# Grouped reads of shared PSUM banks, and a builder's clock that knows of bank turns

## The chip, the cores and the metric

The kernel runs on one core of one Trainium2 chip. The metric is the device time of one execution in microseconds (us). On a core, TensorE (PE; its weight loads are PEld), VectorE (DVE), ScalarE (ACT) and GpSimd (POOL) each work through their own list of instructions in order and wait for one another by semaphores; SyncE (SP) issues transfers. Matmul results land in PSUM, eight banks, from where only ACT and DVE read them.

## What is computed

One step of a decoder layer with two mixers on the same input: 256 prompt tokens and 8 sequences of 8 sample tokens, 320 columns in all, model width 2048.

```
h   = rms_norm(x) * (1 + scale) + shift            # scale, shift, gate from c @ w_ada
a_qkv, a_z, ..., b_z, i_q, ..., g_a, g_b = split(h @ w_in)
y_a = rms_norm(gated_delta_rule(conv(a_qkv))) * silu(a_z)       # 32 heads, states of 128 x 128
y_b = attend(q, k, v, top-k of an indexer) * silu(b_z)          # 16 heads, paged cache for the samples
out = rms_norm((sigmoid(g_a) * (y_a @ w_pa) + sigmoid(g_b) * (y_b @ w_pb)) @ w_out)
y   = x + gate * out

# the delta rule, chunk by chunk (128 tokens in the kernel, two chunks of prompt):
u = u_c - w_c @ s;   o = qd_c @ s + qk_c @ u;   s = s * g_tail + k_tail^T @ u
```

## The kernel before

**The stream.** All large products are weight-stationary. A weight matrix is loaded in tiles `raw` of 1024 rows by 256 columns (three buffers, issued on SP). A *unit* is 128 columns of one such half: ACT rounds it into `whi` (L334), DVE subtracts to get `wlo` (L335), three buffers of each, and PE runs 24 matmuls of 320 columns into one of two banks `pm`: input high part by `whi`, low part by `whi`, high part by `wlo`, for eight row blocks. Two units make a block of 128 output channels, and its `..._done` function reads the bank. The stream runs in the order: indexer queries, queries, gate `b_z`, gate `g_a`, then eight groups for the delta rule (keys, queries, `a_z`, values), gate `g_b`, and the three output projections.

**Side work.** Everything else is a Python generator ("side"). The other six banks, `ps`, are a ring that the sides take and give back; in the delta-rule stage one of them holds the short convolution. `stream` calls `side_round` twice in each unit, after 12 and after 24 matmuls (L364, L370), and each side whose time has come issues one step. The instructions of a step go to the end of each engine's list at that moment, so the order of the calls is the order on every engine.

**The clock.** When a side's time has come is decided by `Clock`, a table of estimated times that the builder keeps while it emits instructions. `Clock.enter` gives each instruction a start, the latest of its engine's time, its inputs' writers and its output's users, and an end. A step's end is stored with the side; `side_round` steps it again when the estimated time of PE has passed it:

```
if side[1] <= clock.t["tensor"]:
    self.step(side)
```

So a cost that the clock leaves out makes a step come early in the program, and PE then waits for it on the chip.

**Waits for a bank.** The framework under the kernel sets the semaphores. Between an ACT instruction and a DVE instruction on the same bank it sets one also where both only read, and where they read different columns.

**The places.** In `prompt_chain` (one for each of 16 pairs of heads) five blocks follow one another, each with a bank of its own: (1) `XT` by `vt[0]`, read by ACT into `wf` (a part of `vt`) and by DVE into `wt` (a tile `w`), for two heads v; (2) the state `S1` (also a tile `w`) and an output `ot`, read by ACT; (3) `kq` by `S1`, read by DVE into `x1` (a part of `vt`) and by ACT into `ot`; (4) `XT` by `x1`, read as in (1); (5) the new state. `sample_chain` has a block like (1) whose bank is read by DVE into `wt` and by ACT into `ot`, and then 16 DVE instructions, each shown as `S<-S,gtr,ps`. The chains of two pairs of heads run side by side. `bz_done` reads a `pm` bank twice, by DVE into `u` and by ACT (tanh) into `t`; both are tiles `t`. At that time DVE also runs the samples' top-k on `scs`, 32 rounds of two instructions. `out_done` reads its bank by ACT into `gsx`, by DVE into the rest of `gsx`, and by ACT into `sqx`. A PE row `pm<-...` belongs to the stream, `ps<-...` to the sides. All instructions go through one helper and carry its line, L56.

Of the kernel before, what the change touches and what calls it, by code (L numbers as in the profile page):

```python
# [11 lines left out]
AF = mybir.ActivationFunctionType  # L12
OP = mybir.AluOpType
AX = mybir.AxisListType
MEM = bass.MemoryType
# [5 lines left out]
NT = NP + NS  # L21
# [46 lines left out]
class Clock:  # L68
# [2 lines left out]

    def __init__(self):
        self.t = dict.fromkeys(("tensor", "vector", "scalar", "gpsimd", "sync", "dma"), 0.0)
        self.written, self.used = {}, {}
        self.last = 0.0

    @staticmethod
# [70 lines left out]
    def enter(self, name, op, args, kw):  # L148
        out = args[0] if args else kw["out"]
        rest = list(args[1:]) + list(kw.values())  # L150
        ins = [a for a in rest if hasattr(a, "tensor") and a is not out and a is not kw.get("accum_out")]
        outs = [out] + ([kw["accum_out"]] if kw.get("accum_out") is not None else [])
        if op == "transpose":
            ins = ins[:1]
        own = None if "dma" in op else name
        start = max(self.t[name], self.ready(*ins, name=own))
        if "dma" not in op or out.space != MEM.DRAM:
            start = max(start, self.idle(*outs, name=own))
        if "dma" in op:
            side = out if out.space != MEM.DRAM else ins[0]  # L160
            rows = self.free(side) // min(out.shape[-1], ins[0].shape[-1])
            size = side.shape[0] * rows * max(512, 4 * min(out.shape[-1], ins[0].shape[-1]))
            self.t[name] = start + (1.0 if name == "gpsimd" else 0.55)
            self.t["dma"] = max(self.t["dma"], start) + size / 3.2e5
            end = max(self.t["dma"], start) + 2.2
        else:
            if kw.get("op") == OP.pow or OP.pow in rest:
                took = 1.6
            else:
                took = self.cost(name, op, outs, ins)  # L170
            end = self.t[name] = start + took
            end += 0.2 if name == "tensor" else 0.1
        by = "dma" if "dma" in op else name
        for a in ins:
            self.note(self.used, a, by, end)
        for a in outs:
            self.note(self.written, a, by, end)
        self.last = max(self.last, end)
# [12 lines left out]
class Kernel:  # L191
# [809 lines left out]
    def bz_done(self, p, h):  # L1001
        self.force(lambda: h in self.att and len(self.t_r.free) >= 2)
        u, t = self.t_r.get(), self.t_r.get()
        self.ts(u, p[:, :NT], 0.5, None, OP.mult)
        self.act(t, p[:, :NT], AF.Tanh, scale=0.5)
        y = self.ybuf[:, h, :]
        self.stt(y[:, NP:NT], t[:, NP:NT], 1.0, u[:, NP:NT], OP.add, OP.mult)
        self.stt(u[:, 0:NP], t[:, 0:NP], 1.0, u[:, 0:NP], OP.add, OP.mult)
        self.tt(y[:, 0:NP], y[:, 0:NP], u[:, 0:NP], OP.mult)
        self.t_r.put(u)  # L1010
        self.t_r.put(t)
        if h == KB - 1:
            self.flags.add("bz")
# [730 lines left out]
    def prompt_chain(self, h, G):  # L1744
        nc, o = self.nc, self.o
        e, hv, K = h % 2, 2 * h, self.K[h]
        while "T" not in G or "vt" not in K:
            yield
        kq, vt, kt, XT, PT = K["kq"], K["vt"], K["ktok"], G["XT"], K["PT"]
        s, stl = self.scal(G, e)  # L1750
        yield self.ready(vt, XT)
        yield from self.need(self.ps_side)
        yield from self.need(self.w, 2)
        if "ot" not in K:
            yield from self.need(self.ot)
            K["ot"] = self.ot.get()
        ot = K["ot"]
        wt, S1 = self.w.get(), self.w.get()
        wf, x1 = vt[:, 0], vt[:, 1]
        p = self.psum()  # L1760
        for v in range(2):
            self.mm(p[:, 128 * v:128 * v + 128], XT[:, 4 * e + 2 * v, :], vt[:, 0, v, :])
        for v in range(2):
            self.act(wf[:, v, :], p[:, 128 * v:128 * v + 128], AF.Copy, scale=s(v, 0))
            self.ts(wt[:, v, :], p[:, 128 * v:128 * v + 128], stl(v, 0), None, OP.mult)
        self.ps_side.put(p)
        yield
        yield from self.need(self.ps_side)
        p = self.psum()
        self.mm(p[:, 0:256], kt[:, 0, :], wt)  # L1770
        for v in range(2):
            self.mm(p[:, 256 + 128 * v:384 + 128 * v], PT[:, v, 0, :], wf[:, v, :])
        self.act(S1, p[:, 0:256].rearrange("p (v d) -> p v d", v=2))
        self.act(ot[:, 0], p[:, 256:512].rearrange("p (v d) -> p v d", v=2))
        self.ps_side.put(p)
        yield
        yield from self.need(self.ps_side)
        p = self.psum()
        self.mm(p[:, 0:256], kq[:, 0, 128:256], S1)
        self.mm(p[:, 256:512], kq[:, 1, 128:256], S1)  # L1780
        for v in range(2):
            hc = hv + v
            self.stt(x1[:, v, :], p[:, 128 * v:128 * v + 128], self.neG[:, 1, hc:hc + 1], vt[:, 1, v, :], OP.mult, OP.add)
            self.act(ot[:, 1, v, :], p[:, 256 + 128 * v:384 + 128 * v], AF.Copy, scale=self.eG[:, 1, hc:hc + 1])
        self.ps_side.put(p)
        yield
        yield from self.need(self.ps_side)
        p = self.psum()
        for v in range(2):
            self.mm(p[:, 128 * v:128 * v + 128], XT[:, 4 * e + 2 * v + 1, :], x1[:, v, :])  # L1790
        for v in range(2):
            self.act(x1[:, v, :], p[:, 128 * v:128 * v + 128], AF.Copy, scale=s(v, 1))
            self.ts(wt[:, v, :], p[:, 128 * v:128 * v + 128], stl(v, 1), None, OP.mult)
        self.ps_side.put(p)
        yield
        yield from self.need(self.ps_side)
        p = self.psum()
        self.mm(p[:, 0:256], kt[:, 1, :], wt)
        for v in range(2):
            self.mm(p[:, 256 + 128 * v:384 + 128 * v], PT[:, v, 1, :], x1[:, v, :])  # L1800
        for v in range(2):
            self.stt(S1[:, v, :], S1[:, v, :], self.gtp[:, 1, hv + v:hv + v + 1], p[:, 128 * v:128 * v + 128],
                     OP.mult, OP.add)
        self.tt(ot[:, 1], p[:, 256:512].rearrange("p (v d) -> p v d", v=2), ot[:, 1], OP.add)
        self.ps_side.put(p)
        self.PT.put(PT)
        self.store(o[5][0, 0, hv:hv + 2].rearrange("h k v -> k h v"), S1, self.w)
        self.w.put(wt)
        self.drop_vt(K)
        self.drop_T(G)  # L1810
        K["P"] = True
# [6 lines left out]
    def sample_chain(self, h, G):  # L1818
# [11 lines left out]
        s, stl = self.scal(G, e)  # L1830
# [20 lines left out]
        p = self.psum()  # L1851
        for v in range(2):
            self.mm(p[:, 128 * v:128 * v + 128], XT[:, 8 + 2 * e + v, :], xr[:, v, :])
        for v in range(2):
            self.ts(wt[:, v, :], p[:, 128 * v:128 * v + 128], stl(v, 2), None, OP.mult)
        self.act(ot[:, 2], p[:, 0:256].rearrange("p (v d) -> p v d", v=2))
        self.ps_side.put(p)
        self.drop_T(G)
        yield
# [199 lines left out]
    def out_done(self, p, k):  # L2059
        self.force(lambda: self.gsx.free and self.sqx.free)  # L2060
        g, s = self.gsx.get(), self.sqx.get()
        self.act(g[:, :NP], p[:, :NP], AF.Copy, scale=self.gatp[:, k, 0:1])
        self.tt(g[:, NP:NT].rearrange("p (b t) -> p b t", t=TS), p[:, NP:NT].rearrange("p (b t) -> p b t", t=TS),
                self.gatp[:, k, 1:9].rearrange("p (b o) -> p b o", o=1).to_broadcast([128, NB, TS]), OP.mult)
        self.act(s, p[:, :NT], AF.Square)

        def gen():
            yield self.ready(g, s)
            p = self.psum()
            for t in range(3):  # L2070
                n = 128 if t < 2 else 64
                self.mm(self.pss[:n, t:t + 1], s[:, 128 * t:128 * t + n], self.one, start=(k == 0 and t == 0),
                        stop=(k == KB - 1), skip=True)
                self.tr(p[:n, 128 * t:128 * t + 128], g[:, 128 * t:128 * t + n])
            for t in range(3):
                n = 128 if t < 2 else 64
                self.act(self.gt[t][:n, 128 * k:128 * (k + 1)], p[:n, 128 * t:128 * t + 128])
            self.ps_side.put(p)
            self.gsx.put(g)
            self.sqx.put(s)  # L2080
            yield
        self.spawn(gen())
# [52 lines left out]
```

## Time and profile before

| | us |
|---|---|
| median of 3 runs | 2323.8 (2316.94 to 2326.34) |
| the profiled execution, device time | 2320.82 |
| its span, first to last instruction | 2319.1 |
| PE idle in the span (2319.1 less 2216.6 busy) | 102.5 |

The times above are of whole executions; all trace times are from the start of the span. Three matmuls of the stream are in flight at a time, so that each is shown longer (0.31 us) than the distance to the next (0.15 us). In a list of waits, `PE ps <- ACT w` means: a PE instruction that writes a `ps` bank was held, and the last thing it waited for was an ACT instruction that writes a tile `w`.

### The profile page before, as it was taken

The page shows a single profiled execution, that of the slowest core. Times are in us where ns is not written, and L with a number is a line of the kernel's source. Part 1 is how long each engine was busy: PE and PEld are TensorE (multiplying, and loading weights), DVE is VectorE, ACT ScalarE, POOL GpSimd, SP SyncE. Part 2 cuts the span into 40 slices and gives each one's busy share as a digit, 9 for nine tenths or more (in the row PEclk, how much of TensorE's full clock was granted, in tenths as well). Part 3 has the DMA queues.
Part 4 walks back from the last instruction along what each step waited for, and adds up shares of the span by engine and source line. Part 5 has one row for each costly group of instructions (what it writes and reads, how often), then busy time and mean ns, then how long its engine had stood idle before and what let it go on. Part 6 is the DMA issues. An engine that isn't in the chain of part 4 may idle for free.

```text
span 2319.1 us, 41332 instructions
## 1 busy us (share of the span) xinstructions
PE 2216.6 (96%) x16448; PEld 2081.1 (90%) x16448; DVE 1368.6 (59%) x2666; ACT 1013.4 (44%) x2191; POOL 469.4 (20%) x624
## 2 busy tenths in 40 slices
PE   5779999999999999999999999999999999999997
PEld 2658997999988999898989898989899999999997
DVE  2323345788844467685868586858665554545433
ACT  2123346443333354554556464546553543333342
POOL 0010000000000007072627162727171000000000
PEclk9878999999999999999999999999999999999999
DMA  9958743434455556475756565656574866644443
GB/s 324 323 162 257 236 162 104 165 110 134 149 202 197 195 177 210 131 237 146 225 169 205 165 208 169 205 168 206 165 231 142 273 210 198 196 153 156 159 142 103
DMA packets 475137, 432.96 MB, mean 187 GB/s; under 512 B 65912, under 2 KB 463880, under 8 KB 472576
## 3 DMA queue, kind: packets, MB, share of 16 engines
q1 hardware_dynamic: 470560, 406.61, 56.3%
q0 software_dynamic: 3840, 21.02, 2.5%
q8 instruction: 129, 2.11, 0.4%
q10 hardware_dynamic: 544, 2.70, 0.3%
q14 instruction: 64, 0.52, 0.1%
HBM read 382.10 MB, written 47.89 MB: 185 GB/s over the span
## 4 chain that ended last, share of the span: by engine, by line
PE 80%; DVE 10%; ACT 4%; POOL 2%; DMA 2%; issue 2%; DVEq 0%; SPq 0%; POOLq 0%; ACTq 0%
PE pm L56 65%; PE ps L56 15%; DVE S L56 2%; DVE wlo L56 2%; DVE ps L56 1%; POOL X L56 1%; ACT whi L56 1%; POOL tmpx L56 1%; DMA raw<-in_w_ada_dram 1%; DMA rawx<-in_w_ada_dram 1%; ACT ot L56 1%; DVE st L56 1%; DVE w L56 1%; DVE awl L56 1%; ACT ps L56 1%
## 5 line engine op out<-in xcount | busy, mean ns | idle before, releaser
L56 PE MATMUL pm<-xh,whi 128*128 128x320 f32 x3328 | 1065.6, 320 | 3.9 <-ACT whi L56 3.9
L56 PE MATMUL pm<-xh,wlo 128*128 128x320 f32 x3328 | 1033.4, 311 | 12.2 <-DVE wlo L56 12.1
L56 PE MATMUL pm<-xl,whi 128*128 128x320 f32 x3328 | 1031.2, 310 | 0.0
L56 DVE TENSOR_TENSOR wlo<-raw,whi 128x1024 fp32r<-128x1024 f32 x480 | 601.9, 1258 | 372.7 <-ACT whi L56 370.9
L56 PEld LDWEIGHTS pm<-xh,whi 128*128 128x128 f32 x3328 | 628.7, 189 | 35.4 <-issue 25.6
L56 PEld LDWEIGHTS pm<-xh,wlo 128*128 128x128 f32 x3328 | 627.9, 189 | 15.2 <-DVE wlo L56 15.0
L56 PEld LDWEIGHTS pm<-xl,whi 128*128 128x128 f32 x3328 | 628.8, 189 | 1.0
L56 ACT ACTIVATE whi<-raw 128x1024 fp32r<-128x1024 f32 x480 | 504.2, 1056 | 261.8 <-PE pm L56 227.5
L56 POOL TENSOR_TENSOR X<-X,tmpx 48x31 f32<-48x31 f32 (+15 forms) x248 | 182.8, 737 | 19.4
L56 POOL TENSOR_TENSOR tmpx<-blk,X 48x31 f32<-48x31 f32 (+15 forms) x248 | 170.7, 688 | 44.3 <-DMA blk<-d_b 25.8
L56 PE MATMUL pm<-y1h,wlo 128*128 128x320 f32 x512 | 157.9, 308 | 0.7 <-DVE wlo L56 0.7
L56 PE MATMUL pm<-y1l,whi 128*128 128x320 f32 x512 | 157.9, 308 | 0.1
L56 PE MATMUL pm<-y1h,whi 128*128 128x320 f32 x512 | 158.0, 309 | 0.0
L56 POOL TENSOR_TENSOR sc<-sc,mh 128x6 f32<-128x6 f32 (+1 forms) x24 | 42.4, 1766 | 438.7 <-DVE sc L56 425.0
L56 DVE SCALAR_TENSOR_TENSOR ps<-xp,cs,ps 128x344 f32<-128x344 f32 x192 | 111.5, 581 | 6.8
L56 POOL TENSOR_TENSOR rfin<-rfin,mh 128x3 f32<-128x3 f32 x1 | 0.8, 850 | 496.2 <-DVE rfin L56 496.2
L56 PEld LDWEIGHTS pm<-y1h,wlo 128*128 128x128 f32 x512 | 96.0, 187 | 1.0 <-DVE wlo L56 1.0
L56 PEld LDWEIGHTS pm<-y1l,whi 128*128 128x128 f32 x512 | 95.9, 187 | 0.3 <-DVE y1l L56 0.3
L56 PEld LDWEIGHTS pm<-y1h,whi 128*128 128x128 f32 x512 | 96.0, 187 | 0.3 <-ACT y1h L56 0.2
L56 ACT ACTIVATE vt<-ps,sc 128x128 f32<-128x128 f32 (+1 forms) x112 | 42.5, 410 | 81.7 <-DVE w L56 64.9
L56 DVE SCALAR_TENSOR_TENSOR S<-S,gtr,ps 128x128 f32<-128x128 f32 x256 | 67.5, 342 | 0.7 <-PE ps L56 0.4
L56 ACT ACTIVATE xp<-pm 128x256 f32<-128x256 f32 (+1 forms) x128 | 31.9, 302 | 71.7 <-PE pm L56 71.5
(310 smaller groups left out, 2332.7 us busy)
## 6 DMA issues: line engine op xcount, KB each, us to landing
raw<-in_w_in_dram SPq DMA_DIRECT2D x176, 1024.0 KB
raw<-in_w_pa_dram SPq DMA_DIRECT2D x32, 1024.0 KB
rawx<-in_w_ada_dram SPq DMA_DIRECT2D x17, 1024.0 KB
a<-in_w_ada_dram SPq DMA_DIRECT2D x16, 1024.0 KB
S<-in_state_gdn_dram SPq DMA_DIRECT2D x32, 512.0 KB
out_dram<-S SPq DMA_DIRECT2D x32, 512.0 KB
raw<-in_w_pb_dram SPq DMA_DIRECT2D x16, 1024.0 KB
raw<-in_w_out_dram SPq DMA_DIRECT2D x16, 1024.0 KB
```

Source lines behind the costliest of these rows:

```text
L56: made = fn(*args, **kw)
```

## The change

In four functions the instructions that read one bank are put in another order, so that all of ACT's come before all of DVE's; nothing is added or left out. In the clock, an ACT or DVE instruction on a bank now also starts no earlier than the other engine's latest end on this bank.

```
@@ Clock.enter
+        if name in ("vector", "scalar"):
+            banks = {a.tensor.name for a in outs + ins if a.space == MEM.PSUM}
+            for b in banks:
+                start = max([start] + [t for e, t in self.bank.get(b, {}).items() if e != name])
...
+        if name in ("vector", "scalar"):
+            for b in banks:
+                self.bank.setdefault(b, {})[name] = end
@@ bz_done
+        self.act(t, p[:, :NT], AF.Tanh, scale=0.5)
         self.ts(u, p[:, :NT], 0.5, None, OP.mult)
-        self.act(t, p[:, :NT], AF.Tanh, scale=0.5)
@@ prompt_chain, block 1 (block 4 likewise, with x1)
         for v in range(2):
             self.act(wf[:, v, :], p[:, 128 * v:128 * v + 128], AF.Copy, scale=s(v, 0))
+        for v in range(2):
             self.ts(wt[:, v, :], p[:, 128 * v:128 * v + 128], stl(v, 0), None, OP.mult)
@@ prompt_chain, block 3
         for v in range(2):
-            hc = hv + v
-            self.stt(x1[:, v, :], p[:, 128 * v:128 * v + 128], self.neG[:, 1, hc:hc + 1], vt[:, 1, v, :], OP.mult, OP.add)
-            self.act(ot[:, 1, v, :], p[:, 256 + 128 * v:384 + 128 * v], AF.Copy, scale=self.eG[:, 1, hc:hc + 1])
+            self.act(ot[:, 1, v, :], p[:, 256 + 128 * v:384 + 128 * v], AF.Copy, scale=self.eG[:, 1, hv + v:hv + v + 1])
+        for v in range(2):
+            self.stt(x1[:, v, :], p[:, 128 * v:128 * v + 128], self.neG[:, 1, hv + v:hv + v + 1], vt[:, 1, v, :],
+                     OP.mult, OP.add)
@@ sample_chain
+        self.act(ot[:, 2], p[:, 0:256].rearrange("p (v d) -> p v d", v=2))
         for v in range(2):
             self.ts(wt[:, v, :], p[:, 128 * v:128 * v + 128], stl(v, 2), None, OP.mult)
-        self.act(ot[:, 2], p[:, 0:256].rearrange("p (v d) -> p v d", v=2))
@@ out_done
         self.act(g[:, :NP], p[:, :NP], AF.Copy, scale=self.gatp[:, k, 0:1])
+        self.act(s, p[:, :NT], AF.Square)
         self.tt(g[:, NP:NT]..., p[:, NP:NT]..., self.gatp[:, k, 1:9]..., OP.mult)
-        self.act(s, p[:, :NT], AF.Square)
```

**ACT, delta-rule stage, third group of heads.** The first `vt` row and its successor are block 4 of one chain, `w` is `S1` of the chain beside it, the second `ot<-ps` is the sample chain's. Before:

```order
L56 ACTIVATE xp_6311<-cs_100 128x8x3
L56 ACTIVATE vt_6346<-ps_70,sc_6361 128x128 [waits PE_49]
L56 ACTIVATE vt_6346<-ps_70,sc_6361 128x128 [waits DVE_49]
L56 ACTIVATE w_6353<-ps_71 128x256 [waits PE_49]
L56 ACTIVATE ot_6356<-ps_71 128x256
L56 ACTIVATE ot_6356<-ps_72 128x256 [waits DVE_49]
L56 ACTIVATE whi_79<-raw_77 128x1024 [waits DMAHW2_49,Activation_49]
```

and now:

```order
L56 ACTIVATE xp_6311<-cs_100 128x8x3
L56 ACTIVATE vt_6346<-ps_70,sc_6361 128x128 [waits DVE_49,PE_49]
L56 ACTIVATE vt_6346<-ps_70,sc_6361 128x128 [waits DVE_49]
L56 ACTIVATE w_6353<-ps_71 128x256 [waits DVE_49,PE_49]
L56 ACTIVATE ot_6356<-ps_71 128x256
L56 ACTIVATE ot_6356<-ps_72 128x256 [waits DVE_49,PE_49]
L56 ACTIVATE whi_79<-raw_77 128x1024 [waits DMAHW2_49,Activation_49]
```

The order is the same; the waits differ. In block 4 ACT overwrites `x1`, which DVE wrote in block 3, so by the code both `vt` rows still have to wait for DVE, each for the older instruction that wrote its half of `x1`; the wait for DVE's read of this bank is what the new order of the source takes away.

**DVE, the same place.** `w_6349` is `wt` of block 4, `w_6351` that of the sample chain, the first `vt` row after them is block 3 of the chain beside. Before:

```order
L56 COPY ct_6344<-xp_6311 128x27 [waits Activation_49]
L56 TENSOR_SCALAR ps_68<-xp_6311,cs_100 128x344 [waits Activation_49]
L56 SCALAR_TENSOR_TENSOR ps_68<-xp_6311,cs_100,ps_68 128x344 [waits DVE_49] x3
L56 TENSOR_SCALAR w_6349<-ps_70,sc_6361 128x128 [waits Activation_49] x2
L56 TENSOR_SCALAR w_6351<-ps_72,sc_6361 128x128 [waits DMAHW4_49,PE_49]
L56 TENSOR_SCALAR w_6351<-ps_72,sc_6361 128x128
L56 TENSOR_TENSOR wlo_82<-raw_77,whi_79 128x1024 [waits DMAHW2_49,Activation_49]
L56 SCALAR_TENSOR_TENSOR vt_6347<-ps_67,neG,vt_6347 128x128 [waits PE_49]
L56 SCALAR_TENSOR_TENSOR vt_6347<-ps_67,neG,vt_6347 128x128 [waits Activation_49]
```

and now:

```order
L56 COPY ct_6344<-xp_6311 128x27 [waits Activation_49]
L56 TENSOR_SCALAR ps_68<-xp_6311,cs_100 128x344 [waits Activation_49]
L56 SCALAR_TENSOR_TENSOR ps_68<-xp_6311,cs_100,ps_68 128x344 [waits DVE_49] x3
L56 TENSOR_SCALAR w_6349<-ps_70,sc_6361 128x128 [waits Activation_49]
L56 TENSOR_SCALAR w_6349<-ps_70,sc_6361 128x128
L56 TENSOR_SCALAR w_6351<-ps_72,sc_6361 128x128 [waits DMAHW4_49,Activation_49]
L56 TENSOR_SCALAR w_6351<-ps_72,sc_6361 128x128
L56 TENSOR_TENSOR wlo_82<-raw_77,whi_79 128x1024 [waits DMAHW2_49,Activation_49]
L56 SCALAR_TENSOR_TENSOR vt_6347<-ps_67,neG,vt_6347 128x128 [waits PE_49,Activation_49]
L56 SCALAR_TENSOR_TENSOR vt_6347<-ps_67,neG,vt_6347 128x128
```

Here too only the waits moved: of each pair the first row waits for ACT, the second for nothing.

**DVE at the gate `b_z`, with the top-k of the samples** (`t<-pm` is `u`, the row after it the product with the tanh). Before:

```order
L56 MAX st_1055<-scs 64x8
L56 MATCH_REPLACE scs<-st_1055,scs 64x1088 [waits DVE_49]
L56 COPY ybuf<-ps_67 128x256 [waits PE_49]
L56 TENSOR_TENSOR wlo_83<-raw_75,whi_80 128x1024 [waits DMAHW1_49,Activation_49]
L56 TENSOR_SCALAR t_1045<-pm_66 128x320 [waits PE_49]
L56 SCALAR_TENSOR_TENSOR ybuf<-t_1046,t_1045 128x64 [waits Activation_49]
```

and now:

```order
L56 TENSOR_TENSOR wlo_82<-raw_77,whi_79 128x1024 [waits DMAHW0_49,Activation_49]
L56 TENSOR_TENSOR wlo_83<-raw_75,whi_80 128x1024 [waits DMAHW1_49,PE_49,Activation_49]
L56 COPY s_1040<-ps_68 128x384 [waits PE_49]
L56 TENSOR_SCALAR t_1045<-pm_66 128x320 [waits Activation_49]
L56 SCALAR_TENSOR_TENSOR ybuf<-t_1046,t_1045 128x64 [waits DVE_49]
```

The wait between ACT and DVE has turned round, and side steps around it stand in other places.

## Rows read from the trace of the kernel before

**Rows 1.** The page's 40 slices of 58 us, busy tenths

```profile
PE   5779999999999999999999999999999999999997
...
DVE  2323345788844467685868586858665554545433
```

**Rows 2.** Waits of PE, 232 to 2262 us (total us, times, longest us)

```profile
PE ps L56 <- ACT w L56: 12.3, 7, 2.2
PE pm L56 <- DVE wlo L56: 6.5, 8, 2.1
PE ps L56 <- ACT s L56: 2.8, 2, 2.1
PE pm L56 <- ACT whi L56: 2.4, 3, 0.9
...
PE ps L56 <- DVE w L56: 0.9, 3, 0.4
...
```

**Rows 3.** Timeline, 1208.6 to 1217.4 us (start, length, instruction, idle before and releaser)

```profile
1209.38 0.37 ACT L56 ACTIVATE vt<-ps,sc 128x128 f32<-128x128 f32 x1
...
1211.74 1.81 DVE L56 SCALAR_TENSOR_TENSOR ps<-xp,cs,ps 128x344 f32<-128x344 f32 x3
...
1212.05 0.31 PE L56 MATMUL pm<-xh,wlo 128*128 128x320 f32 x1
1213.46 0.35 DVE L56 TENSOR_SCALAR w<-ps,sc 128x128 f32<-128x128 f32 x1
1213.84 0.37 ACT L56 ACTIVATE vt<-ps,sc 128x128 f32<-128x128 f32 x1 [4.10 <-DVE w L56]
1214.11 0.38 ACT L56 ACTIVATE w<-ps 128x256 f32<-128x256 f32 x1
1214.24 0.87 DVE L56 TENSOR_SCALAR w<-ps,sc 128x128 f32<-128x128 f32 x3 [0.43 <-ACT vt L56]
...
1214.54 1.13 PE L56 MATMUL ps<-w,kq 128*128 128x256 f32 x4 [2.17 <-ACT w L56]
...
1217.26 0.38 PE L56 MATMUL ps<-w,ktok 128*128 128x256 f32 x1
```

**Rows 4.** Waits of ACT, 232 to 2262 us

```profile
ACT whi L56 <- PE pm L56: 218.7, 130, 3.1
...
ACT t L56 <- DVE t L56: 65.1, 16, 7.0
ACT vt L56 <- DVE w L56: 64.9, 32, 5.2
```

**Rows 5.** Stretches: length, busy us (instructions) of each engine, PEclk, DMA share, GB/s

```profile
1205.00:1208.00 3.00, 3.00 (x28) 2.29 (x27) 2.56 (x8) 0.73 (x2) 0.00 (x0) 1.00 0.30 74
1329.00:1332.40 3.40, 3.40 (x15) 3.31 (x14) 1.84 (x3) 1.43 (x3) 0.00 (x0) 0.50 0.27 78
1479.20:1482.60 3.40, 3.40 (x15) 3.40 (x14) 2.59 (x5) 1.64 (x6) 3.16 (x4) 0.50 0.80 258
```

**Rows 6.** Timeline, 546 to 552 us

```profile
548.96 0.47 DVE L56 TENSOR_SCALAR t<-pm 128x320 f32<-128x320 f32 x1
549.46 0.44 ACT L56 ACTIVATE t<-pm 128x320 f32<-128x320 f32 x1 [5.25 <-DVE t L56]
549.80 1.05 ACT L56 ACTIVATE whi<-raw 128x1024 fp32r<-128x1024 f32 x1
...
551.16 0.59 PE L56 MATMUL ps<-ident,s 128*128 128x128 f32 x2 [2.09 <-ACT s L56]
```

**Rows 7.** Timeline, 2303.9 to 2306 us

```profile
2304.20 0.47 ACT L56 ACTIVATE gsx<-pm,gatp 128x256 f32<-128x256 f32 x1 [4.74 <-PE pm L56]
...
2304.97 0.44 ACT L56 ACTIVATE sqx<-pm 128x320 f32<-128x320 f32 x1 [0.29 <-DVE rfin L56]
...
2305.46 0.38 PE L56 MATMUL ps<-one,sqx 128*128 128x1 f32 x2 [1.35 <-ACT sqx L56]
```

**Rows 8.** The page's costliest groups, POOL (count, busy us, mean ns)

```profile
L56 POOL TENSOR_TENSOR X<-X,tmpx 48x31 f32<-48x31 f32 (+15 forms) x248 | 182.8, 737 | 19.4
```

More of the change, by code (lines that the diff above doesn't have):

```diff
@@ L73, in __init__ @@
         self.t = dict.fromkeys(("tensor", "vector", "scalar", "gpsimd", "sync", "dma"), 0.0)
-        self.written, self.used = {}, {}
+        self.written, self.used, self.bank = {}, {}, {}
         self.last = 0.0
@@ L1792, in prompt_chain @@
             self.act(x1[:, v, :], p[:, 128 * v:128 * v + 128], AF.Copy, scale=s(v, 1))
+        for v in range(2):
             self.ts(wt[:, v, :], p[:, 128 * v:128 * v + 128], stl(v, 1), None, OP.mult)
```

## Prediction

> **What bounds the kernel now.** I read the slices first: PE is full in all but the first three and the last [rows 1], and no instruction of PE is added or removed. So the change can only give back PE's idle time, or add to it. The first 232 us keep their order (the order of PE differs first after 1164 matmuls of the stream, in the query projection), and the end is a fixed tail. The second view is therefore the list of PE's waits between 232 and 2262 us [rows 2]. Its five largest of the kinds that matter here are 12.3, 6.5, 2.8, 2.4 and 0.9 us, 24.9 us in all. The largest is a wait for ACT to write `S1`, 7 times; the third a wait for ACT to write the attention's `s`, twice. Third, the timelines around one of each show why ACT was late.
>
> In the delta-rule stage [rows 3], ACT reads the first half of block 4 at 1209.38 and is then held for 4.10 us: its second half must wait for DVE's read of the first, and DVE has 16 state updates and a convolution ahead of it (the last three convolution rows alone take 1.81 us from 1211.74) and comes only at 1213.46. `S1` of the other chain stands behind that held read and is written at 1214.11. PE ended its 12 stream matmuls with the row at 1212.05 and idled 2.17 us. So it is not the amount of work on ACT or DVE that PE pays for, but one turn at a bank that ties ACT's queue to DVE's. Over the run ACT loses 64.9 us in 32 such turns [rows 4]; PE feels 7 of them.
>
> At the gate `b_z` [rows 6] it is the same: the tanh waits 5.25 us for DVE's read of the same bank, which stands behind the top-k, and the two `s` reads behind the tanh let PE idle 2.09 us. All 16 tanh waits make 65.1 us on ACT [rows 4].
>
> **The change part by part.** The sum is made against the profiled execution, 2320.8 us (its span is 2319.1), which is 3.0 us under the median of the runs, 2323.8; I add the 3.0 at the end.
>
> *Blocks 1 and 4.* ACT's second read no longer waits for DVE. In [rows 3] it would follow the first by 0.27 us (the distance of the ACT rows at 1213.84 and 1214.11). PE issued the product that `S1` reads before those 12 matmuls, which are 0.15 us apart, so before 1210.40; `S1` is then written by about 1210.9, while PE asks for it at 1212.05 + 0.15 = 1212.20. All 7 waits should go: -12.3 us. What is late next is `wt` of block 4 for block 5. PE reached that step 1217.26 - 1214.54 = 2.72 us after `kq`, so it will now at 1214.92. DVE's own run up to 1213.46 does not shift, but its rows then follow at 0.87 / 3 = 0.29 us instead of losing 0.43 us to a turn; both halves are there at 1213.46 + 0.29 + 0.35 = 1214.10. There are 0.8 us to spare, and I cost this at nothing; if the cover were gone, each of the 7 places would return up to the 1.2 us of one more `wlo` in front, less the 0.8.
>
> *The clock of PE.* Three stretches of 3.4 us at half the granted clock begin right behind such a wait (at 1329, 1561 and 1674 us; one is shown), and PE issues 15 instructions in one where 28 fit into 3.0 us at full clock [rows 5]. Each costs 1.7 us: -5.1 us. A fourth, at 1479, follows a wait for `wlo` and is left standing.
>
> *`bz_done`.* ACT's tanh comes at once, and DVE's `u`, as late as before, finds ACT long done. The two waits for `s` go: -2.8 us. Behind the new wait on DVE stand the top-k and `wlo`; ACT would have to be more than 5 us late for it to count.
>
> *Block 3, the sample chain.* Here the first DVE product now comes behind ACT's reads, up to 0.37 + 0.27 us later, the second about as before. PE takes both halves together and waited for DVE's `w` 0.9 us in all [rows 2]: nothing to 1 us, I take 0.
>
> *`out_done`.* Steady blocks are hidden by 7 us of stream matmuls each. At the very end the third read waits for DVE's: 2304.97, which is 0.77 us after the first; behind a 320-column read ACT's next row follows 0.34 us later [rows 6], so PE's 2305.46 [rows 7] comes some 0.4 us sooner: -0.4.
>
> *The moved side steps.* This is what the trace of before cannot show. With the new estimates, steps of the query and `b_z` stages and everything after about 5300 of the stream's 11,520 matmuls are spread anew, on SP and POOL too. The other waits, 6.5 for `wlo` and 2.4 for `whi` [rows 2], come of such chance collisions. They could vanish (-8.9, and the fourth clock dip, -1.7) or double (+8.9). On SP some weight loads change places with small loads and stores; the cover is that `whi` usually waits for PE to free its buffer, 130 times, and not for data [rows 4]. On POOL a norm's power now stands in one place behind four more steps of the triangular inverse; with the partner of each `X` instruction about as long as it (737 ns, [rows 8]) that is 4 x 2 x 0.74 = 5.9 us later, and the DVE row that takes the result would hold `wlo` for as much; in that stage DVE is 5 to 8 tenths busy [rows 1], so part of it would be made up. I take +3 us, a third of what doubling would cost, because estimates that know of one more wait should make early steps rarer, not more frequent.
>
> *Against grouping* speaks a rule of the Trainium skill, page Perfetto Trace Analysis, section Optimizing Scalar/DVE Operations: where ScalarE and VectorE are not saturated but cause bubbles elsewhere, breaking work up may let it complete sooner. Alternating halves is such a breaking up. By the rule the products that DVE makes would come later for it; by [rows 2] PE waits for them hardly at all, and the sum stays.
>
> Sum: -12.3 - 5.1 - 2.8 - 0.4 + 3 = -17.6. 2320.8 - 17.6 = 2303.2, and with 3.0 us from profiled run to median 2306.2. Bounds: -8.9 - 1.7 instead of +3 gives 2292.6, +8.9 gives 2312.1.
>
> **Rivals.**
>
> *The gain is eaten.* PE comes earlier to every step, DVE does not: it is the engine that set the 4.10 us, and it still runs its 16 updates and a convolution before `w`. If the waits for `S1` turn half into waits for `wt` or for a bank that DVE has not yet read, 6 us return, the dips of the clock stay (5.1), and the spread costs its 3: 2323.8 - 12.3 - 2.8 - 0.4 + 6 + 3 = 2317. For it: the 0.8 us to spare is less than one `wlo`. Against it: DVE loses its own turns too.
>
> *DVE in line behind ACT, slower.* At 64 places in the chains (16 chains, three blocks and the sample's) DVE's first read now waits until ACT has done both. Where ACT is held by a `whi` that waits for PE, as it is 130 times for 218.7 us, or 1.7 us each [rows 4], DVE stands too, with `wlo` behind it, and PE waits for `wlo` in the end. Each such place costs 1.7 us; the 20.6 us of terms above are used up at 12 places, and at 20 the time is 2323.8 - 20.6 + 34 = 2337. For it: DVE is busy 8 tenths in the `b_z` stretch and in many slices of the delta rule [rows 1], so lost time there is not made up. Against it: DVE's list has the `wlo` of that same `whi` ahead of block 3's reads where I looked, so it would have stood anyway. The rule of the Trainium skill named above (Perfetto Trace Analysis, Optimizing Scalar/DVE Operations) points the same way as this rival.
>
> *More than the sum.* The better estimates also clear the waits for `wlo` and `whi` and the fourth dip: 2293, worked out above.
>
> **How the numbers follow.** The forecast 0.60, with its own range 2300 to 2314; eaten 0.25; slower 0.08; more 0.07. About 0.5%, 11.6 us, is what a measurement of this kernel can tell from no change, so faster is under 2312.2. Of the forecast 0.57 lies under it, with "more" 0.64. Same: 0.03 of the forecast and all of "eaten", 0.28. Slower 0.08. The range 2295 to 2322 leaves out "slower", a tenth of "eaten" and half of "more", some 0.15.
>
> **What would show it.** Right: PE's waits for ACT `w` gone or under 2 us, ACT's waits for DVE `w` and `t` small, no half-clock stretch behind `kq`, the end of the stream 16 to 20 us sooner. Wrong: as many microseconds of PE waits under other names (DVE `w`, `wlo`, ACT `ot`), or DVE rows `w` and `vt` with idle time before them that ACT ends.

## The result, and the profile after

The changed kernel takes 2295.18 us (median of 4 runs, 2294.81 to 2298.58) beside 2321.32 us of the kernel before: ratio 0.9893, 95% interval 0.9876 to 0.9910. Timed twice more it gave 0.9889 (0.9872 to 0.9907) and 0.9879 (0.9862 to 0.9897). That is faster, as predicted, but by some 25 us and not by 17.6.

The spans (2319.1 and 2296.9 us) differ by 22.2 us, though the first stream matmul came 4.9 us later in this execution, behind the first loads (169.82 and 174.68 us), which the change does not touch. A measure without that part of the noise is the *stream time*, from the start of the first stream matmul to the start of the last: 2133.98 us before, 2107.35 after, 26.6 us less. It is used below, though it has noise of its own: in three profiles of the changed kernel it ran from 2106.6 to 2113.4 us.

The page's slices of the changed kernel, 57.4 us each:

```profile
PE   5778999999999999999999999999999999999997
PEclk8878999999999999999999999999999999999999
```

Waits of PE, 232 to 2262 us, changed kernel (total us, times, longest):

```profile
PE pm L56 <- DVE wlo L56: 7.8, 10, 1.8
PE ps L56 <- DMA cst<-in_state_conv_dram: 1.7, 2, 1.5
PE ps L56 <- DMA a<-in_cache_k_dram,idx: 1.4, 2, 1.2
PE ps L56 <- DVE S L56: 0.8, 3, 0.3
PE ps L56 <- DVE ot L56: 0.6, 1, 0.6
```

Of [rows 2] the waits for ACT `w`, ACT `s`, ACT `whi` and DVE `w` are all gone. Those for `wlo` are larger (6.5 before; 7.5 and 7.4 in two further profiles of the change), and two loads are new: PE meets a gather and a small load before they have landed. The small load's wait stands in all three profiles (1.7, 2.0 and 1.9 us). The gather's does not (1.4, 0.2, none), and the reads alone, timed again with the old places of the steps (see the experiments), have one too (0.6), so it can't be laid to the new places. No stretch at half clock lies between 190 us and the tail in this profile; there were four.

The place of [rows 3] in the changed kernel (timeline; start, length, instruction, idle before and releaser):

```profile
1206.15 0.63 ACT L56 ACTIVATE vt<-ps,sc 128x128 f32<-128x128 f32 x2
...
1206.97 0.38 ACT L56 ACTIVATE w<-ps 128x256 f32<-128x256 f32 x1 [0.20 <-PE ps L56]
1207.26 0.66 ACT L56 ACTIVATE ot<-ps 128x256 f32<-128x256 f32 x2
1207.78 1.07 ACT L56 ACTIVATE whi<-raw 128x1024 fp32r<-128x1024 f32 x1
...
1208.64 1.81 DVE L56 SCALAR_TENSOR_TENSOR ps<-xp,cs,ps 128x344 f32<-128x344 f32 x3
...
1208.97 1.02 PE L56 MATMUL ps<-w,kq 128*128 128x256 f32 x4
...
1210.36 1.12 DVE L56 TENSOR_SCALAR w<-ps,sc 128x128 f32<-128x128 f32 x4
...
1211.59 0.59 PE L56 MATMUL ps<-w,ktok 128*128 128x256 f32 x2
```

ACT reads both halves in one row of 0.63 us, and `S1` starts 0.82 us behind the first read; the sample chain's `ot` (the second of the two `ot` rows) and `whi` follow at once, while DVE is still in its state updates and its convolution; PE's `kq` waits for nothing. DVE's two `wt` of this chain are the first two of four rows that start 0.26 us apart, so the second (0.35 us long) ends at about 1210.97; PE asks for it at 1211.59, 0.6 us later.

The gate `b_z` [rows 6] and the tail [rows 7] after:

```profile
549.86 0.44 ACT L56 ACTIVATE t<-pm 128x320 f32<-128x320 f32 x1
...
550.33 0.49 DVE L56 TENSOR_SCALAR t<-pm 128x320 f32<-128x320 f32 x1 [0.16 <-ACT t L56]
...
2282.76 0.43 ACT L56 ACTIVATE sqx<-pm 128x320 f32<-128x320 f32 x1
...
2283.24 0.38 PE L56 MATMUL ps<-one,sqx 128*128 128x1 f32 x2 [0.89 <-ACT sqx L56]
```

The tanh waits for nothing now (5.25 us before), and PE's wait at the end is 0.89 us and not 1.35.

ACT's waits for DVE `t` and `vt`'s for DVE `w` [rows 4], 130 us together, have no row any more. What the new order costs DVE shows in its own list of waits, 232 to 2262 us:

```profile
DVE w L56 <- ACT ot L56: 15.1, 7, 3.0
```

In return its waits of `w` for ACT `vt` fell from 23.0 to 11.9 us, and PE's list above has no wait for `w`.

### The profile page after: what moved, and what is told of

The parts are those of the page before. It is cut to its first block, busy times and chain, and to the rows that moved or that the text cites. A ratio compares the mean times of both kernels' runs of the same rounds, so it can differ in the third digit from the quotient of the medians.

```text
span 2296.9 us, 41417 instructions
## 1 busy us (share of the span) xinstructions
PE 2210.2 (96%) x16448; PEld 2079.9 (91%) x16448; DVE 1361.3 (59%) x2666; ACT 1010.3 (44%) x2191; POOL 469.6 (20%) x624
## 4 chain that ended last, share of the span: by engine, by line
PE 80%; DVE 9%; DMA 4%; ACT 3%; POOL 2%; issue 1%; DVEq 0%; SPq 0%; POOLq 0%; ACTq 0%
PE pm L56 64%; PE ps L56 16%; DVE wlo L56 2%; DMA rawx<-in_w_ada_dram 1%; DVE ps L56 1%; DVE S L56 1%; POOL X L56 1%; POOL tmpx L56 1%; ACT whi L56 1%; DMA a<-in_cache_k_dram,idx 1%; ACT ps L56 1%; ACT ot L56 1%; DMA cst<-in_state_conv_dram 1%; DVE awl L56 1%; DVE st L56 0%
## 5 line engine op out<-in xcount | busy, mean ns | idle before, releaser
L56 PEld LDWEIGHTS pm<-xh,whi 128*128 128x128 f32 x3328 | 626.6, 188 | 32.1 <-issue 25.6
L56 POOL TENSOR_TENSOR tmpx<-blk,X 48x31 f32<-48x31 f32 (+15 forms) x248 | 180.6, 728 | 40.5 <-DMA blk<-d_b 22.1
L56 POOL DMA_INDIRECT a<-in_cache_v_dram,idx x8 | 7.5, 936 | 251.9 <-DVE st L56 224.5
```

Source lines behind the costliest of these rows:

```text
L56: made = fn(*args, **kw)
```

## The experiments

Theory A: ACT's queue, held at the turns of a bank, is what PE paid for. Rival B: the new places of the side steps, which the new clock brings, make the gain. Rival C: DVE now loses more behind ACT than ACT gains. Later runs split theory A: which of the turns, and whether their number counts (rival D) or who goes first.

In all kernels but those with the new clock or its places, every engine's list of instructions stands word for word as in the kernel before; only the waits between ACT and DVE differ.

| kernel | median us | before, same chip | ratio (95%) | stream time us |
|---|---|---|---|---|
| reads alone | 2292.45 | 2323.81 | 0.9855 (0.9835 to 0.9876) | 2102.4 |
| places of the steps alone | 2327.40 | 2323.81 | 1.0022 (1.0011 to 1.0033) | 2140.1 |
| clock alone | 2321.47 | 2323.81 | 0.9994 (0.9985 to 1.0004) | 2130.6 |
| blocks 1, 4 | 2316.99 | 2323.81 | 0.9967 (0.9954 to 0.9980) | 2124.2 |
| blocks 1, 3, 4, DVE first | 2322.38 | 2322.05 | 0.9997 (0.9983 to 1.0010) | 2133.8 |
| blocks 1, 3, 4, ACT first | 2307.94 | 2322.05 | 0.9945 (0.9929 to 0.9961) | 2119.5 |
| blocks 1, 4, sample chain | 2299.96 | 2322.05 | 0.9907 (0.9886 to 0.9929) | 2112.3 |
| sample chain | 2319.38 | 2321.68 | 0.9989 (0.9976 to 1.0001) | 2130.3 |
| reads alone, again | 2291.13 | 2321.68 | 0.9868 (0.9852 to 0.9884) | 2104.0 |
| change, again | 2297.85 | 2322.05 | 0.9889 (0.9872 to 0.9907) | 2113.4 |
| change, third | 2295.28 | 2321.68 | 0.9879 (0.9862 to 0.9897) | 2106.6 |

**Reads alone.** The diff of the change without its two pieces in `Clock`.

> The kernel before with the new order of the reads in all four functions, and with its old clock; every engine's list of instructions stays word for word in its old order, only the waits between ACT and DVE change. Theory A (ACT's queue, held at the turns of a bank, is what PE paid for): the terms of the sum that need no new step order, 12.3 + 2.8 + 0.4 and three clock dips of 1.7, go: some 20 us faster than before, about 2301, and PE's waits for ACT w and ACT s are gone. Rival B (the new places of the side steps made the gain): within 5 us of before. Rival C (DVE now stands behind ACT): slower than before, with DVE idle before w and vt.

Measured: 31 us faster, more than the whole change and half as much again as the 20 us that were expected. Theory A stands; B and C fall. Its waits of PE, 232 to 2262 us:

```profile
PE pm L56 <- DVE wlo L56: 4.0, 5, 1.4
PE pm L56 <- ACT whi L56: 1.4, 2, 0.9
PE ps L56 <- DVE ot L56: 0.6, 1, 0.6
```

Since PE's list is the same, its 16,448 rows can be laid beside those of before one by one, and each step in the distance of their starts has a place. From the first stream matmul to the last, 31.6 us are gained: 16.8 at the seven waits for `S1`, 3.8 at the gate, and 11.0 elsewhere. Of these 11.0 some 7 lie at waits for `wlo` and `whi`, some 4 at `ps` rows that waited for `ot`, `w` or `S`, a new stretch at half clock takes 1.5 back, and the rest is small.

**Places of the steps alone.** Old order of reads; each choice to issue a step or a load is replayed from the changed kernel's build.

```
-            if side[1] <= clock.t["tensor"]:
+            if PLAN.due(side[1] <= clock.t["tensor"]):   # the recorded choice
                 self.step(side)
```

> The kernel before with its old order of reads, but each side step, and each weight load, is issued at the place where the changed kernel issues it (the choices of that build are replayed). Theory A: the turns of the banks still hold ACT, so most of PE's waits for ACT w and ACT s stay, some 10 us or more: at most 6 us faster than before, 2315 to 2323. Rival B: 15 us faster or more, under 2308, with few waits for ACT w left.

Measured: 5 us slower than before by the ratio (3.6 by the medians). By themselves the new places give nothing; PE's waits for `S1` stay, those for `wlo` double (6.5 before):

```profile
PE pm L56 <- DVE wlo L56: 13.7, 14, 2.4
PE ps L56 <- ACT w L56: 11.2, 7, 2.2
```

**Clock alone.** The two pieces in `Clock`, nothing else.

> The old order of reads with the new clock alone: the builder knows what a turn at a bank costs and places the steps later by it. Theory A: the turns still hold ACT on the chip, the later steps hide a part of them: 0 to 10 us faster than before. Rival B: as fast as the changed kernel, about 2295, since the estimates are what counts.

Measured: no difference. Yet the waits for `S1` are gone from its list; waits of about the same size came under other names, at later steps of the chains:

```profile
PE pm L56 <- DVE wlo L56: 11.7, 12, 1.6
PE ps L56 <- DVE ot L56: 5.8, 4, 2.8
PE ps L56 <- DVE S L56: 4.9, 3, 2.3
```

**Blocks 1 and 4.** Only the two hunks that split the loop over v in these blocks.

> Only blocks 1 and 4 of the prompt chains read in the new order, old clock, all lists in their old order. By the sum of the prediction -12.3 for the seven waits for S1 and -5.1 for three clock dips, 17.4 us faster than before, about 2304. If the hold of ACT in block 3 or at the sample chain takes their place (the gain is eaten), 5 to 10 us faster.

Measured: 2323.81 x 0.0033 = 7.7 us faster, not 17.4. All waits for `S1` are gone; those for `ot` rise from 1.6 to 10.1 us. The place of [rows 3] in this kernel (timeline):

```profile
1211.24 1.12 DVE L56 TENSOR_SCALAR w<-ps,sc 128x128 f32<-128x128 f32 x4
1212.40 0.38 ACT L56 ACTIVATE ot<-ps 128x256 f32<-128x256 f32 x1 [3.76 <-DVE w L56]
...
1212.68 1.05 ACT L56 ACTIVATE whi<-raw 128x1024 fp32r<-128x1024 f32 x1
...
1213.76 1.23 DVE L56 TENSOR_TENSOR wlo<-raw,whi 128x1024 fp32r<-128x1024 f32 x1 [1.40 <-ACT whi L56]
1214.90 0.35 DVE L56 SCALAR_TENSOR_TENSOR vt<-ps,neG,vt 128x128 f32<-128x128 f32 x1
1215.28 0.37 ACT L56 ACTIVATE ot<-ps,eG 128x128 f32<-128x128 f32 x1 [1.56 <-DVE vt L56]
1215.68 0.35 DVE L56 SCALAR_TENSOR_TENSOR vt<-ps,neG,vt 128x128 f32<-128x128 f32 x1 [0.43 <-ACT ot L56]
...
1216.07 0.37 ACT L56 ACTIVATE ot<-ps,eG 128x128 f32<-128x128 f32 x1 [0.42 <-DVE vt L56]
...
1216.49 1.12 PE L56 MATMUL ps<-w,ktok 32*128 32x256 f32 x10 [2.21 <-ACT ot L56]
```

The hold only moved two rows down ACT's list. The sample chain's read stands there for 3.76 us behind DVE's `w`; `whi` comes only behind it, at 1212.68; DVE idles for `whi`, block 3 of the chain beside it comes after that `wlo`, the last three of its four reads each wait for the one before, and PE loses 2.21 us, as much as at `S1` before.

**Blocks 1, 3 and 4, DVE first.** In blocks 1 and 4 (block 3 likewise):

```
         for v in range(2):
-            self.act(wf[:, v, :], p[:, 128 * v:128 * v + 128], AF.Copy, scale=s(v, 0))
             self.ts(wt[:, v, :], p[:, 128 * v:128 * v + 128], stl(v, 0), None, OP.mult)
+        for v in range(2):
+            self.act(wf[:, v, :], p[:, 128 * v:128 * v + 128], AF.Copy, scale=s(v, 0))
```

> Blocks 1, 3 and 4 of the prompt chains grouped the other way: all of DVE's reads first, then all of ACT's; the gate b_z, the sample chain and the output as in the kernel before, all lists in their old order. As many turns are saved as with ACT first. Theory A (the harm is that ACT, with whi and S1 queued behind, stands in line behind DVE): ACT's first read now waits for DVE too, S1 comes as late as before, 0 to 5 us faster than before or even slower. Rival D (each turn saved is what counts, whoever is first): as fast as the same three blocks with ACT first.

Measured: nothing gained. Waits of PE, and of ACT, 232 to 2262 us:

```profile
PE ps L56 <- ACT w L56: 16.4, 7, 2.8
```

```profile
ACT vt L56 <- DVE w L56: 76.5, 27, 6.4
```

There are fewer turns (27 waits where there were 32), but each is longer, and ACT loses 76.5 us and not 64.9. Rival D falls: it counts which engine goes first, not how often the bank changes hands. The rule of the Trainium skill that the prediction weighed (Perfetto Trace Analysis, Optimizing Scalar/DVE Operations) says that breaking work up may let it complete sooner; no run here tests that, since every instruction keeps its size and only the order differs. The kernel before, which alternates halves, and this one, which does not, differ by 0.0003.

**Blocks 1, 3 and 4, ACT first.** The hunks of these three blocks from the change.

> Blocks 1, 3 and 4 of the prompt chains grouped with ACT first; sample chain, gate b_z and output as before, all lists in their old order. In the run with blocks 1 and 4 alone PE's lost time came back as waits for ACT ot, 10.1 us, some microseconds behind a read of the sample chain that held ACT for 3.8 us. Theory A1 (the sample chain's turn is what kept the gain): about as that run, 2310 to 2318. Rival A2 (block 3's turns, two of which stand right ahead of that wait, kept it): ten microseconds or more faster than that run, under 2307.

Measured: 2307.94, between the two forecasts, 0.9 us above A2's 2307 and 2.1 below A1's 2310: block 3 counts too. By the ratios it adds some 5 us to blocks 1 and 4 (0.9945 beside 0.9967, on another chip; the intervals touch). The same place (timeline):

```profile
1213.28 0.38 ACT L56 ACTIVATE ot<-ps 128x256 f32<-128x256 f32 x1 [3.88 <-DVE w L56]
...
1215.35 1.07 ACT L56 ACTIVATE whi<-raw 128x1024 fp32r<-128x1024 f32 x1
1215.79 0.60 DVE L56 SCALAR_TENSOR_TENSOR vt<-ps,neG,vt 128x128 f32<-128x128 f32 x2
...
1216.54 1.10 PE L56 MATMUL ps<-w,ktok 32*128 32x256 f32 x10 [1.50 <-ACT whi L56]
```

The sample chain's read still holds ACT, 3.88 us; with block 3 grouped PE loses 1.50 us behind it and not 2.21. The row names `whi` as the releaser, which ends at 1216.42; block 3's DVE rows end at 1216.39. By the code this product does not read `whi` but needs free banks, which speaks for block 3; the trace does not settle it.

**Blocks 1, 4 and the sample chain.** The hunks of blocks 1 and 4 and of `sample_chain`.

> Blocks 1 and 4 and the sample chain grouped with ACT first; block 3, the gate and the output as before, all lists in their old order. Theory A1: most of what all reads together gained in the delta-rule stage, 28 us, is here: about 2298 to 2303. Rival A2: no more than blocks 1 and 4 alone, 2312 to 2318.

Measured: 2299.96, as theory A1 said. PE's waits for `ot` are down to 3.6 us. At that place ACT is now held at block 3's first turn, 3.94 us, and PE waits 0.73 us (list of waits; timeline):

```profile
PE ps L56 <- ACT ot L56: 3.6, 5, 0.7
```

```profile
1209.76 0.37 ACT L56 ACTIVATE ot<-ps,eG 128x128 f32<-128x128 f32 x1 [3.94 <-DVE vt L56]
...
1210.97 1.13 PE L56 MATMUL ps<-w,ktok 32*128 32x256 f32 x10 [0.73 <-ACT ot L56]
```

The rest of the reads (block 3, gate, output) is worth 9.9 us more of stream time (2112.3 less 2102.4), 3.8 of them at the gate; how much of the remainder is block 3's is not separated from the noise.

**The sample chain alone.** The hunk of `sample_chain`.

> Only the sample chain's block reordered (ACT's read ahead of DVE's two), all else and all lists as before. With blocks 1 and 4 alone 7.6 us were gained, with both 21.6 by the ratios. Theory A1 (two holds stand behind one another on ACT's list, and either alone keeps PE waiting): 0 to 4 us faster, the waits for ACT w and the three half-clock stretches stay. Rival (the sample chain's turn was the whole cause): 12 to 15 us faster by itself.

Measured: 2.6 us by the ratio, not separated from nothing. The seven waits for `S1` are as before, with two half-clock stretches behind them where three were expected:

```profile
PE ps L56 <- ACT w L56: 12.2, 7, 2.2
```

So 7.7 us (blocks 1, 4) and 2.6 us (sample chain) apart, but 2322.05 x 0.0093 = 21.6 us together: two holds stand behind one another on ACT's list, and while one is left, PE waits for nearly as long.

**The change beside the reads alone.** Both kernels once more, first the change, then both on one chip.

> The changed kernel itself, beside the others on one chip. If the new clock's places cost what the traces say (reads alone 31.6 us of stream time gained, the change 26.6 us counted from the first matmul of the stream), it is some 5 us slower than the kernel with the reads alone, a ratio of 0.987 to 0.990 to the kernel before. If the difference between the two was only one of runs, its ratio is 0.9855.

> The kernel with the new order of reads and the old clock once more, to stand beside the changed kernel on one chip. Theory A: it stays ahead of the changed kernel by 4 to 9 us, ratio 0.984 to 0.987 to the kernel before, since with the old places of the steps PE meets no gather or small load too early. Rival: both are the same within 2 us, and the difference seen before came of single runs.

> The changed kernel beside the run above: ratio 0.988 to 0.990 to the kernel before by theory A, 4 to 9 us behind the reads alone.

Measured: on one chip the reads alone are 4.2 us ahead (2291.13 and 2295.28), but the intervals of the two ratios overlap. The stream times do not (2102.4 and 2104.0; 2107.4, 2113.4 and 2106.6), which puts the cost of the new places at 3 to 11 us; with two and three profiles that is likely, not shown. The lists of waits point the same way in every profile: 7.4 to 7.8 us for `wlo` in the change and 4.0 to 4.6 in the reads alone, and 1.7 to 2.0 for the small load beside none. The kernel with the reads alone is the fastest one here, ahead of the kernel before without doubt.

## Why the prediction was right, and where its sum was not

*What bounds the kernel* was read rightly: the waits of PE that ACT's queue makes. The time lies in the range of 2295 to 2322, but by 0.2 us, and it is outside the forecast's own 2300 to 2314; the sum is 7 to 9 us too small (17.6 against some 25 by the ratio, 26.1 by the medians). So the mechanism was right, the size was not, and that the time still fell into the range is in part luck.

*Blocks 1 and 4, -12.3 and -5.1.* The places gave what was foretold, 16.8 us and not 17.4 in the run with the reads alone. Each stall cost a little more than its idle time: the one with 2.17 us of idle and no half-clock stretch cost 2.44. Each half-clock stretch at these places cost less, 3.43 - 2.44 = 1.0 us and not 1.7 (the one that was new in the reads alone cost 1.5). The 0.8 us to spare for `wt` was 0.6. But the term was put down to the wrong edit: these blocks alone gave 7.7 us.

*Block 3 and the sample chain, 0.* This is the step that failed. The prediction looked at what PE waits for in [rows 2], and there these turns are hardly to be seen, because block 4's turn stood ahead of them on ACT and did the waiting. Before, the sample chain's read waits 0.39 us, and the product for which PE loses 2.21 us with blocks 1 and 4 alone waits 0.31 us (timeline):

```profile
1215.15 0.38 ACT L56 ACTIVATE ot<-ps 128x256 f32<-128x256 f32 x1 [0.39 <-DVE w L56]
...
1219.24 1.12 PE L56 MATMUL ps<-w,ktok 32*128 32x256 f32 x10 [0.31 <-ACT ot L56]
```

That second wait belongs to a row of PE's list (232 to 2262 us) that the prediction's five largest left out, though it is larger than the last of them:

```profile
PE ps L56 <- ACT ot L56: 1.6, 3, 0.7
```

Where block 4's turn is taken away, the sample chain's is next, 3.76 us, and behind that block 3's, 3.94 us; in the sum they were safe only because the change takes them all away. Behind blocks 1 and 4 the sample chain's hunk is worth some 14 us (21.6 less 7.7) and block 3's some 5, where the sum had 0 for both. What was asked of `wt`, "what is late next", was not asked of ACT's own list.

*The moved side steps, +3.* The sign likely holds, and the size is that or more: 3 to 11 us by stream times. What was wrong is the cover of this term. The waits for `wlo` and `whi` were taken as chance collisions of steps, and bounded as such; with every list unchanged, 11.0 us of these and of smaller `ps` waits went with the reads, so they hung on the order of the reads. The way that the rows of blocks 1 and 4 alone show (ACT held, `whi` late, `wlo` late, PE waits) fits them, but it was not followed at each; at the 0.70 us for `wlo` at 1845.60 us ACT had last waited 2.32 us for a load, and why that wait went too stays open. The sum by these runs: -16.8 - 3.8 - 11.0 - 0.5 = -32.1 for the reads, and 5.0 back for the places (2107.4 less 2102.4): -27.1.

*The gate, -2.8:* 3.8 in the run with the reads alone. The two stalls of 0.68 and 2.09 us cost 1.05 and 2.45, and a wait for `whi` between them shrank by 0.35. *The tail, -0.4:* 0.46 (1.352 less 0.891).

*The rivals.* "More than the sum" came nearest in time (2293), though not by its mechanism: the better estimates did not clear the waits for `wlo`, the reads did. "The gain is eaten" did not happen to the change, but blocks 1 and 4 alone show it happening, by ACT's next holds and not by a late `wt`. "DVE in line behind ACT" shows in DVE's list, 15.1 us behind `ot` as the prediction's last paragraph named it, and, with the reads alone, in no wait of PE that grew.

## What to carry to other kernels

Where two engines read one bank, let the one go first behind which the critical queue stands; grouping with the other first was worth nothing here. When a hold is to be removed from a queue, walk down that queue and find the next hold before pricing the first: the list of waits shows only the one that ends last. And price a hold by all that is queued behind it (here `whi`, and `wlo` after that), not by the wait that bears its name.

## What the runs showed of the hardware

The half-clock stretches of PE are not fixed to a kernel: the changed one had none in its first profile, three in its second and none in its third. All 24 in the thirteen profiles (from 190 us to the tail) begin inside a stall of PE or within 1.4 us of its end, but not each stall has one. One place shows it best: the same two waits, for `whi` and `wlo`, 1.3 us apart (0.93 and 0.71 us before, at 1061.66 and 1062.92), stand in ten of the profiles, and a half-clock stretch goes with them in five. Stretches (length, busy us and instructions of PE, PEld, DVE, ACT, POOL, PEclk, DMA share, GB/s), first of the changed kernel's second profile, then of blocks 1 and 4 alone, right behind the 2.21 us:

```profile
1060.30:1063.70 3.40, 3.40 (x15) 3.40 (x14) 2.14 (x2) 0.69 (x1) 0.00 (x0) 0.50 0.44 94
818.00:821.40 3.40, 3.40 (x15) 3.40 (x14) 0.61 (x2) 1.15 (x4) 0.00 (x0) 0.50 0.46 133
```

```profile
1216.50:1219.90 3.40, 3.40 (x27) 3.03 (x28) 3.04 (x13) 3.24 (x13) 0.00 (x0) 1.00 0.13 39
```

In the first two PE ran at 1.2 GHz, in the third, behind a longer stall, at 2.4. So a term for the clock, as in the prediction's -5.1, is a chance and not a sum of places. A turn at a bank costs the engine that waits 0.42 to 0.43 us where the other engine is ready, hardly more than the other's read of 0.35 to 0.37 us (the rows of blocks 1 and 4 alone at 1215.68 and 1216.07): dear is not the turn but what the other engine has queued ahead of it.
